# Modulation products placed further behind their loads, and two small jobs moved from VectorE to ScalarE

## The chip, the core and the metric

The kernel runs on one core of a Trainium2 chip. Its engines are TensorE (PE in the rows, with PEld for the loading of its weights), VectorE (DVE), ScalarE (ACT), GpSimd (POOL) and SyncE (SP, whose queue issues the DMAs). The time is in microseconds (us) on the device, from one launch; lower is better.

## The reference

Two layers of a backbone over T = 640 tokens (128 of context and 512 of latents) at width 1024. Each layer modulates a normalised input, mixes tokens by three branches, merges them by gates, and then runs a SwiGLU FFN, modulated in the same way. What matters here are the modulation and one branch:

```python
m = silu(c) @ w_mod[l] + b_mod[l]           # 6 x 1024 columns: shift, scale, gate, twice (adaLN)

def step(s, inp):                            # gated DeltaNet, chunks of 64, forward and backward
    qi, ki, kgi, u, w, ... = inp             # u, w come from the inverse of a triangular matrix
    v_new = u - w @ s                        # product with the state, scaled by a decay
    o = q_scaled @ s + (attn of the chunk) @ v_new
    s = s * decay + ki^T @ v_new
```

There are two copies of the modulation (for context and latents), and the recurrence runs in both directions over the chunks.

## The kernel before

All products are fp32, split in a high and a low part: each weight tile is loaded by SP (`wr`), cast to its high part on ScalarE (`wh`), the rest is taken on GpSimd (`wl`), and TensorE runs three matmuls a product into a PSUM tile `pg`. A matmul of this kind covers 320 tokens. A count of "matmul rows" below is a count of these.

**The order is written by a model clock.** The program is a Python generator that emits all engines' instructions in one pass. Main work (the matmul rows) is emitted as it comes; side work (adaLN products, the inverses and scans of the DeltaNet) stands in coroutines. Each coroutine has a time `cur.t`, from a model of every engine's clock (`tick`), and `pump` emits the next piece of a coroutine between two pieces of main work once the model's TensorE clock plus a hint has reached that time (line 435). A DMA in the model takes its bytes by 3.6e5 a us and 2 us. The engines then run their queues in the order emitted, each in order, with semaphores between them. Most instructions are recorded at one line, L2175, that of the helper that emits them.

**adaLN products** (`mods`, line 686). The first 16 columns' products of layer 0 run at the start of the program. All later ones come in 40 halves: one 1 MB load of `in_wmod` into one tile `S` (in the rows `A<-in_wmod_dram`), then 16 rows of small products (`ps<-A,ct`, 32 matmuls in the trace). Because there is one tile, a half's load can start only when the half before has been read. After two halves ScalarE copies the row out, and `turn` turns it by one matmul (`128x8`) and adds the bias on VectorE. The halves lie at six places: layer 0 columns 16 to 28 (74 to 120 us of the span), 28 to 40 (beside the last scan steps, 543 to 586), 40 to 48 (886 to 910), layer 1 columns 0 to 32 (1030 to 1140), 32 to 40 (1952 to 1979), 40 to 48 (2278 to 2300).

**The inverse** (`delta_inv`) is done per batch on VectorE by eliminating columns one after another (`A<-A` with 128 partitions), with `STREAM_TRANSPOSE` to bring 32x32 blocks in place; small matmuls on TensorE (`ps<-A,A 32x32`) then join the blocks. Batch 0 of each layer is "mixed" (it holds both directions), and for each of its four quarters three copies of 32x256 exchange the blocks, in the same tiles `Nm`, `B`, `X` (lines 1319 to 1321).

**The scan** (`delta_step`, line 1365 on) runs 9 steps a layer with an earlier state. Each multiplies queries and keys by the state `S` on TensorE (`ps<-S,A`, two PSUM tiles), scales both by a decay (`egc`, in the rows `dex`): the first tile by one VectorE instruction of 128x512, the second by four ScalarE activations of 128x128. VectorE then subtracts from the values into `R` (two of 128x256, `A<-A,U`), TensorE multiplies `R` by the inverse (`ps<-A` 64x64), and so on to the new state. The order puts 12 matmul rows between the product with the state and the product of `R`.

**The Hyena branch** runs beside the inverses: its projections go from PSUM through ScalarE (`T<-pg`) to VectorE's convolution (`T<-T,par,T` 128x641), and to DRAM (`hyS<-T`).

Of the kernel before, what the change touches and what calls it, by code (L numbers as in the profile page):

```python
# [12 lines left out]
AF = mybir.ActivationFunctionType  # L13
ALU = mybir.AluOpType
# [4 lines left out]
P = 128  # L19
# [279 lines left out]
class _Net:  # L299
# [386 lines left out]
    def mods(self, l, lo, hi, par=False, hint=0.5, first=False):  # L686

        nc = self.nc  # L690
        if par:
            self.load_par(l)
        if l not in self.mod:
            self.mod[l] = self.p2.tile([P, 2, 48], F32, tag="mod", name=self.nm("mod"))
        mv = self.mod[l]
        pick = self.ident.rearrange("p (g c) -> p g c", g=4)[:, :, 0:2]
        last = None

        def turn(j, row):
            ps = self.ps()  # L700
            nc.tensor.matmul(ps[:, 0:8], row, pick, start=True, stop=True)
            nc.vector.tensor_tensor(out=mv[:, :, j:j + 4], in0=ps[:, 0:8].rearrange("p (g s) -> p s g", g=4),
                                    in1=self.par[l][0][:, None, C_BMOD + j:C_BMOD + j + 4].to_broadcast([P, 2, 4]),
                                    op=ALU.add)

        def add(ps, w, h):
            for k in range(KD // 2):
                for g in range(4):
                    nc.tensor.matmul(ps[32 * g:32 * g + 32, :P], self.ct[4 * h + k], w[g][:, k * P:k * P + P],
                                     start=h + k == 0, stop=h == 1 and k == 3)  # L710

        W = {}
        if first:
            for j in range(lo, hi, 2):
                S = self.A()
                for i in range(2):
                    if j + i == hi - 4:
                        self.wload(1)
                    W[j + i] = S[:, i * D:i * D + D]
                    nc.sync.dma_start(W[j + i], self.I["wmod"][l, j + i])  # L720
        else:
            S = self.A()
        for j in range(lo, hi, 4):
            ps = None
            for h in range(2):
                if first:
                    w = [W[j + g][:, h * 512:h * 512 + 512] for g in range(4)]
                else:
                    w = [S[:, g * 512:g * 512 + 512] for g in range(4)]
                    nc.sync.dma_start(S[:, :2048].rearrange("p (g c) -> p g c", g=4),  # L730
                                      self.I["wmod"][l, j:j + 4, :, h * 512:h * 512 + 512].rearrange("g p c -> p g c"))
                self.on(*w, *([last[1]] if last else []))
                yield hint
                if first and j == lo and not h:
                    self.tables()
                ps = ps or self.ps()
                add(ps, w, h)
                if last:
                    turn(*last)
                    last = None  # L740
            row = self.U()[:, :P]
            nc.scalar.copy(row, ps[:, :P])
            last = j, row
        self.on(last[1])
        yield hint
        turn(*last)
# [506 lines left out]
    def delta_inv(self, N, us):  # L1253

        nc = self.nc
        v = nc.vector
# [32 lines left out]
        for c in range(31, 0, -1):  # L1289
            js = [(c, 32)] if c > 24 else [(c, c + (32 - c) // 2), (c + (32 - c) // 2, 32)]  # L1290
            tv = []
            for a, b in js:
# [3 lines left out]
                                in1=X[:, c:c + 1, a:b].to_broadcast([P, c, w]), op=ALU.mult)  # L1296
# [6 lines left out]
        def unpack(dst, p, a, o2):  # L1303
            q = slice(64 * p + 32 * a, 64 * p + 32 * a + 32)
            src = X[q].rearrange("p r c -> p c r") if not o2 else X[q]
            v.transpose(out=dst.rearrange("p m i -> p i m"), in_=src)

        for p, a in quads:
            q = slice(64 * p + 32 * a, 64 * p + 32 * a + 32)
            bwd = p ^ us[0]  # L1310
            nd = Nm[q, :, 32 * a:32 * a + 32]
            if mixed:
                unpack(nd, p, a, 0)
                yield 1.5
                unpack(B[q], p, a, 1)
                ub = [u for u in range(nu) if p ^ us[u]][0]
                b3 = X[q, 0:8]
                bv, nv = B[q, ub * 8:ub * 8 + 8], nd[:, ub * 8:ub * 8 + 8]
                v.tensor_copy(b3, nv)
                v.tensor_copy(nv, bv)  # L1320
                v.tensor_copy(bv, b3)
            else:
                unpack(nd, p, a, bwd)
                if a == bwd:
                    yield 1.5
                    unpack(B[q], p, a, 1 - bwd)
            yield 0 if (p, a) == quads[-1] else 1.5

        W = S[:, 1024:2048].rearrange("p (m c) -> p m c", c=32)
        for m0 in range(0, nu * 8, 16):  # L1330
            ps = self.ps()
            for m in range(m0, m0 + 16):
                s = us[m // 8]
# [7 lines left out]
            for mm in range(m0, m0 + 16, 8 if mixed else 16):  # L1341
                n = 8 if mixed else 16
                s = us[mm // 8]
# [5 lines left out]
        for m0 in range(0, nu * 8, 16):  # L1349
            ps = self.ps()  # L1350
            for m in range(m0, m0 + 16):
                s = us[m // 8]
# [6 lines left out]
            for mm in range(m0, m0 + 16, 8 if mixed else 16):  # L1359
                n = 8 if mixed else 16  # L1360
                s = us[mm // 8]
# [8 lines left out]
    def delta_step(self, N, Pm, R, St, u, s, t, S, zero):  # L1370

        nc = self.nc
        v = nc.vector
# [8 lines left out]
        if not zero:  # L1382
            pk = [self.ps(), self.ps()]
            for hh in range(4):
                for n, src in enumerate((self.k, self.q)):
                    for h2, par in DIAG:
                        c0 = t * P + par * 64
                        nc.tensor.matmul(pk[h2][halves[par], hh * P + n * 64:hh * P + n * 64 + 64],
                                         src[halves[h2], hh, c0:c0 + 64], S[halves[h2], par ^ s, hh],
                                         start=True, stop=True)  # L1390
            tm = [self.U().rearrange("p (a n d) -> p a n d", a=4, n=2) for _ in range(2)]
            v.tensor_tensor(out=tm[0].rearrange("p a n d -> p a (n d)"), in0=pk[0].rearrange("p (a d) -> p a d", a=4),
                            in1=self.egc[:, s, t, 0, :, None].to_broadcast([P, 4, 128]), op=ALU.mult)
            for hh in range(4):
                nc.scalar.activation(tm[1][:, hh].rearrange("p n d -> p (n d)"), pk[1][:, hh * P:hh * P + P], AF.Copy,
                                     scale=self.egc[:, s, t, 1, hh:hh + 1])
            for h2 in range(2):
                v.tensor_tensor(out=R[:, h2], in0=hv(vt)[:, h2], in1=tm[h2][:, :, 0], op=ALU.subtract)
            nc.gpsimd.tensor_tensor(out=St, in0=S, in1=self.egl[:, s, :, t, :, None].to_broadcast([P, 2, 4, 64]),
                                    op=ALU.mult)  # L1400
        else:
            nc.gpsimd.tensor_copy(R, hv(vt))
        nc.gpsimd.tensor_tensor(out=hv(kg), in0=hv(kt), in1=self.kgf[:, s, t, :, :, None].to_broadcast([P, 2, 4, 64]),
                                op=ALU.mult)
# [821 lines left out]
```

## Time and profile before

| | |
|---|---|
| runs | 2827.09, 2834.18, 2837.05 us; median 2834.18 |
| profiled execution | 2837.89 us, of it 2836.1 in the span |
| mean granted TensorE clock | 0.949 |
| TensorE busy | 2566.9 us, 91% |
| VectorE busy | 1856.7 us, 65% |
| ScalarE busy | 1017.8 us, 36% |
| GpSimd busy | 1332.8 us, 47% |

The busy times are of the one profiled execution, over its whole span; the granted clock is a share of TensorE's full 2.4 GHz, and 0.50 is its lower level of 1.2 GHz.

### The profile page before, as it was taken

What the parts mean: (1) busy time and instruction counts of PE and PEld (TensorE: products, weight loads), DVE (VectorE), ACT (ScalarE), POOL (GpSimd) and SP (SyncE); (2) the same over time, 40 slices, a digit from 0 to 9 for tenths busy, and PEclk for the clock granted to TensorE, in tenths of its full rate; (3) what the DMA queues carried; (4) which work ended last, traced back from release to release, by engine and by line L of the source; (5) the groups of instructions that cost most, each with busy time, mean ns of one, the idle gap of its engine ahead of it and who ended that gap; (6) DMA issues with size and microseconds to landing.
All of it is one profiled execution on the core that took longest, in us unless ns stands there. A gap on an engine that the chain in (4) does not pass through costs nothing. (4 is left out here: it accounts for less than half of the span.)

```text
span 2836.1 us, 55639 instructions
## 1 busy us (share of the span) xinstructions
PE 2566.9 (91%) x22520; PEld 2434.9 (86%) x22520; DVE 1856.7 (65%) x3417; ACT 1017.8 (36%) x2175; POOL 1332.8 (47%) x1228
## 2 busy tenths in 40 slices
PE   5898779788999999999988979698899989999998
PEld 3687779788998888999977778687889989999997
DVE  5466987544654484767665789784555347877765
ACT  4454224232332342433435532332323323444432
POOL 2234426242335464666742444353423345767662
PEclk8999989899999999999999989798999999999999
DMA  7541221333564246222222312213336442222222
GB/s 288 178 143 56 69 77 56 115 120 122 180 234 148 84 129 216 91 81 89 84 84 97 121 54 79 78 58 98 115 138 243 152 156 65 71 83 83 82 75 82
DMA packets 109552, 324.18 MB, mean 114 GB/s; under 512 B 10202, under 2 KB 24538, under 8 KB 102816
## 3 DMA queue, kind: packets, MB, share of 16 engines
q1 hardware_dynamic: 107856, 312.76, 32.8%
q0 software_dynamic: 1440, 7.87, 0.8%
q8 instruction: 177, 2.90, 0.4%
q14 instruction: 79, 0.65, 0.1%
HBM read 288.60 MB, written 37.24 MB: 115 GB/s over the span
## 5 line engine op out<-in xcount | busy, mean ns | idle before, releaser
L2175 PE MATMUL pg<-A,wh 128*128 128x320 f32 (+1 forms) x6304 | 1473.2, 321 | 52.2 <-DVE T L2175 15.3
L2175 PEld LDWEIGHTS pg<-A,wh 128*128 128x128 f32 (+1 forms) x6304 | 1082.0, 194 | 98.1 <-POOL A L2175 18.6
L2175 POOL TENSOR_TENSOR wl<-wr,wh 128x512 fp32r<-128x512 f32 (+2 forms) x486 | 680.0, 1413 | 769.6 <-ACT wh L2175 730.7
L2175 PE MATMUL pg<-A,wl 128*128 128x320 f32 (+1 forms) x3152 | 997.7, 317 | 0.3 <-POOL wl L2175 0.2
L2175 PEld LDWEIGHTS pg<-A,wl 128*128 128x128 f32 (+1 forms) x3152 | 610.2, 194 | 3.6 <-POOL wl L2175 2.7
L2175 ACT CAST wh<-wr 128x512 fp32r<-128x512 f32 (+2 forms) x486 | 286.3, 612 | 442.9 <-PE pg L2175 341.4
L2175 PE MATMUL ps<-A,wh 128*128 128x320 f32 x1696 | 378.0, 309 | 0.0
L2175 PEld LDWEIGHTS ps<-A,wh 128*128 128x128 f32 x1696 | 283.4, 188 | 1.4 <-issue 1.2
L2175 PE MATMUL ps<-A,wl 128*128 128x320 f32 x848 | 262.9, 310 | 4.6 <-POOL wl L2175 4.4
L2175 PE MATMUL ps<-A,A 32*32 32x32 f32 (+5 forms) x2984 | 215.1, 251 | 52.9 <-DVE A L2175 51.0
L2175 POOL TENSOR_TENSOR wl<-U,wh 128x512 fp32r<-128x512 f32 x160 | 226.6, 1432 | 48.0 <-ACT wh L2175 48.0
L2175 PEld LDWEIGHTS ps<-A,A 32*32 32x32 f32 (+2 forms) x2984 | 186.4, 154 | 66.3 <-DVE A L2175 52.2
L2175 DVE TENSOR_TENSOR A<-A 128x120 f32<-128x120 f32 (+22 forms) x690 | 216.1, 375 | 11.0 <-DMA A<-hyS 8.0
L2175 DVE TENSOR_TENSOR T<-T,T 128x320 f32<-128x320 f32 (+1 forms) x139 | 130.3, 937 | 86.0 <-ACT T L2175 81.8
L2175 POOL TENSOR_TENSOR A<-A,A 128x640 fp32r<-128x640 f32 (+5 forms) x84 | 121.0, 1453 | 112.5 <-ACT A L2175 111.6
L2175 PEld LDWEIGHTS ps<-A,wl 128*128 128x128 f32 x848 | 159.2, 188 | 7.0 <-POOL wl L2175 7.0
L2175 PE MATMUL pg<-A,A 128*128 128x320 f32 x1056 | 160.9, 310 | 0.0
L2175 ACT CAST wh<-U 128x512 fp32r<-128x512 f32 x160 | 99.1, 620 | 162.8 <-PE ps L2175 64.2
L2175 PEld LDWEIGHTS pg<-A,A 128*128 128x128 f32 x1056 | 156.1, 188 | 0.7 <-issue 0.2
L2175 DVE STREAM_TRANSPOSE A<-A 32x1024 f32<-32x1024 f32 x72 | 148.9, 2093 | 1.3
L2175 DVE TENSOR_TENSOR U<-ps,U 128x512 f32<-128x512 f32 x144 | 78.0, 543 | 104.2 <-PE ps L2175 66.3
L2175 DVE SCALAR_TENSOR_TENSOR A<-pg,mod,A 128x320 f32<-128x320 f32 (+2 forms) x152 | 72.8, 492 | 84.9 <-PE pg L2175 84.6
(163 smaller groups left out, 3021.1 us busy)
## 6 DMA issues: line engine op xcount, KB each, us to landing
wr<-in_wbig_dram SPq DMA_DIRECT2D x272, 512.0 KB, 3.6
A<-in_wmod_dram SPq DMA_DIRECT2D x40, 1024.0 KB, 5.3
A<-hT SPq DMA_DIRECT2D x32, 1024.0 KB, 7.1
kSp<-U SPq DMA_DIRECT2D x40, 256.0 KB, 2.1
U<-kSp SPq DMA_DIRECT2D x40, 256.0 KB, 6.0
A<-in_wmod_dram SPq DMA_DIRECT2D x16, 512.0 KB, 10.2
hyS<-T SPq DMA_DIRECT2D x24, 320.5 KB, 3.1
wr<-in_wbig_dram SPq DMA_DIRECT2D x16, 384.0 KB, 3.2
```

The source lines that it names most:

```text
L2175: return f(*a, **k)
```

## The change

Three edits. In `mods`, each of the 40 later halves gets 4 us added to its coroutine's time after the model's end of its load, so that its products are emitted further behind the load. In `delta_inv`, the three copies per quarter of a mixed batch go from VectorE to ScalarE (24 instructions). In `delta_step`, the VectorE instruction that scales the first PSUM tile becomes four ScalarE activations, so that ScalarE does eight a step (18 VectorE instructions out, 72 ScalarE instructions in).

```diff
@@ mods
                 self.on(*w, *([last[1]] if last else []))
+                if not first:
+                    self.cur.t += 4.0
                 yield hint
@@ delta_inv
-                v.tensor_copy(b3, nv)
-                v.tensor_copy(nv, bv)
-                v.tensor_copy(bv, b3)
+                nc.scalar.copy(b3, nv)
+                nc.scalar.copy(nv, bv)
+                nc.scalar.copy(bv, b3)
@@ delta_step
-            v.tensor_tensor(out=tm[0].rearrange("p a n d -> p a (n d)"), in0=pk[0].rearrange("p (a d) -> p a d", a=4),
-                            in1=self.egc[:, s, t, 0, :, None].to_broadcast([P, 4, 128]), op=ALU.mult)
-            for hh in range(4):
-                nc.scalar.activation(tm[1][:, hh].rearrange("p n d -> p (n d)"), pk[1][:, hh * P:hh * P + P], AF.Copy,
-                                     scale=self.egc[:, s, t, 1, hh:hh + 1])
+            for h2 in range(2):
+                for hh in range(4):
+                    nc.scalar.activation(tm[h2][:, hh].rearrange("p n d -> p (n d)"), pk[h2][:, hh * P:hh * P + P],
+                                         AF.Copy, scale=self.egc[:, s, t, h2, hh:hh + 1])
```

Since the model clock sets the order, all three edits move instructions. Three places show it.

SyncE's queue at layer 0's columns 40 to 48 (886 to 910 us), before: four loads of adaLN weights (`A`) and the stream's weight loads (`wr`).

```order
L2175 DMA wr_9441<-in_wbig_dram 128x1024
L2175 DMA wr_9507<-in_wbig_dram 128x1024
L2175 DMA A_9509<-in_wmod_dram 128x4x512 x2
L2175 DMA wr_9603<-in_wbig_dram 128x1024
L2175 DMA A_9509<-in_wmod_dram 128x4x512 x2
L2175 DMA wr_9727<-in_wbig_dram 128x1024
```

The same place after the change.

```order
L2176 DMA A_9536<-in_wmod_dram 128x4x512
L2176 DMA wr_9627<-in_wbig_dram 128x1024
L2176 DMA A_9536<-in_wmod_dram 128x4x512
L2176 DMA wr_9714<-in_wbig_dram 128x1024
L2176 DMA A_9536<-in_wmod_dram 128x4x512
L2176 DMA wr_9809<-in_wbig_dram 128x1024
L2176 DMA A_9536<-in_wmod_dram 128x4x512
```

Every adaLN load now has a weight load of the stream between it and the next. On TensorE the four halves stood 30, 24 and 24 matmul rows apart and stand 60, 54 and 54 apart; in layer 0's columns 16 to 28 the first three spacings go from 12, 24 and 30 rows to 42, 48 and 78, the last two from 36 and 66 to 30 and 60; in layer 1's columns 0 to 32 they were 24 to 54 and are 54 to 84; at 2278 to 2300 us as at 886, and at 1952 to 1979 us from 18, 6 and 18 to 24, 24 and 24.

TensorE at the end of layer 0's scan, columns 28 to 40, before: `ps<-A,ct` is an adaLN half, `small,U` its `turn`, `pg` the stream's matmuls, `64x64 x16` a product of the scan.

```order
L2175 MATMUL ps_6293<-A_5907,ct 32x128 x16
L2175 MATMUL pg_6446<-A_449,wh_6065 128x320
L2175 MATMUL pg_6446<-A_451,wh_6065 128x320
L2175 MATMUL pg_6446<-A_449,wl_6066 128x320
L2175 MATMUL pg_6446<-A_449,wh_6065 128x320
L2175 MATMUL pg_6446<-A_451,wh_6065 128x320
L2175 MATMUL pg_6446<-A_449,wl_6066 128x320
L2175 MATMUL ps_6453<-A_4379 64x64 x16
L2175 MATMUL ps_6472<-small,U_6444 128x8
L2175 MATMUL pg_6446<-A_449,wh_6065 128x320
```

The same end after the change, from the scan's last product on.

```order
L2176 MATMUL ps_6578<-U_6556,A_4493 64x64 x16
L2176 MATMUL ps_6442<-A_6041,ct 32x128 x16
L2176 MATMUL ps_6618<-A_6041,ct 32x128 x16
L2176 MATMUL ps_6635<-small,U_6615 128x8
L2176 MATMUL ps_6618<-A_6041,ct 32x128 x16
L2176 MATMUL ps_6657<-small,U_6655 128x8
L2176 MATMUL pg_6661<-A_449,wh_6210 128x320
```

The last three of the six halves now stand behind one another with no matmul row between them, behind the scan instead of beside it. Elsewhere in layer 0 the join of batch 0's inverse moves from 1232 matmul rows after the program's start to 1346, that of batch 1 from 1340 to 1400; in layer 1 both stand 18 rows earlier.

ScalarE in layer 0's mixed inverse, before: casts of the weight stream (`wh<-wr`) and evictions of a Hyena projection (`T<-pg`).

```order
L2175 COPY T_3318<-pg_3324 128x192
L2175 ACTIVATE T_3319<-pg_3324,par_90 128x192
L2175 CAST wh_3393<-wr_3236 128x512
L2175 CAST wh_3397<-wr_3236 128x512
L2175 COPY T_3318<-pg_3367 128x320
L2175 ACTIVATE T_3319<-pg_3367,par_90 128x320
```

The same place after the change, at the first quarter.

```order
L2176 COPY T_3404<-pg_3410 128x192
L2176 ACTIVATE T_3405<-pg_3410,par_90 128x192
L2176 COPY A_2544<-A_2321 32x256
L2176 COPY A_2321<-A_2544 32x8x32
L2176 COPY A_2544<-A_2544 32x256
L2176 CAST wh_3483<-wr_3310 128x512
L2176 CAST wh_3487<-wr_3310 128x512
L2176 COPY T_3404<-pg_3454 128x320
L2176 ACTIVATE T_3405<-pg_3454,par_90 128x320
```

The three copies, the first of which waits for VectorE's `STREAM_TRANSPOSE`, now stand ahead of two casts and of the eviction whose result VectorE's next convolution reads. VectorE's own transposes and eliminations of the next quarter wait for none of the copies.

## Rows read from the trace of the kernel before

**Rows 1.** Waits of TensorE, whole run: engine, tile, releaser: total us, times, longest.
```profile
PE ps L2175 <- DVE A L2175: 64.9, 24, 14.5
PE ps L2175 <- DMA A<-in_wmod_dram: 34.5, 23, 4.7
```

**Rows 2.** The same, of windows 74:120, 543:586, 886:910, 1030:1140, 1952:1979, 2278:2300.
```profile
PE ps L2175 <- DMA A<-in_wmod_dram: 4.5, 3, 3.3
...
PE ps L2175 <- DMA A<-in_wmod_dram: 8.9, 3, 4.7
...
PE ps L2175 <- DMA A<-in_wmod_dram: 5.6, 4, 2.3
...
PE ps L2175 <- DMA A<-in_wmod_dram: 6.6, 8, 1.4
...
PE ps L2175 <- DMA A<-in_wmod_dram: 3.0, 1, 3.0
...
PE ps L2175 <- DMA A<-in_wmod_dram: 6.0, 4, 2.7
```

**Rows 3.** Windows: us, busy PE, PEld, DVE, ACT, POOL, PEclk, DMA share, GB/s.
```profile
84.00:86.00 2.00, 2.00 (x15) 2.00 (x14) 0.00 (x0) 0.97 (x3) 1.13 (x1) 0.97 0.86 299
...
1150.00:1450.00 300.00, 299.68 (x2034) 297.68 (x2034) 208.27 (x338) 115.82 (x218) 188.64 (x136) 1.00 0.27 84
...
1970.00:1972.00 2.00, 2.00 (x57) 1.93 (x49) 0.75 (x2) 0.32 (x1) 1.27 (x1) 0.58 0.88 342
```

**Rows 4.** The same view, layer 0's inverse.
```profile
265.00:390.00 125.00, 96.75 (x929) 92.04 (x928) 122.69 (x268) 30.55 (x72) 50.98 (x66) 0.88 0.24 76
```

**Rows 5.** Timeline of TensorE there, the join of batch 0.
```profile
384.40 1.73 PE L2175 MATMUL ps<-A,A 32*32 32x32 f32 x62 [13.16 <-DVE A L2175]
```

**Rows 6.** Timeline, loads (SPq) and products: start, duration, count, [idle before, releaser].
```profile
75.56 0.38 SPq L2175 DMA_DIRECT2D A<-in_wmod_dram  x1
...
80.68 1.94 PE L2175 MATMUL ps<-A,ct 128*32 128x128 f32 x32 [3.31 <-DMA A<-in_wmod_dram]
...
552.58 0.37 SPq L2175 DMA_DIRECT2D A<-in_wmod_dram  x1
...
559.82 1.94 PE L2175 MATMUL ps<-A,ct 128*32 128x128 f32 x32 [4.75 <-DMA A<-in_wmod_dram]
...
1965.27 1.93 PE L2175 MATMUL ps<-A,ct 128*32 128x128 f32 x32 [2.97 <-DMA A<-in_wmod_dram]
```

**Rows 7.** Lines by form, whole run (`wh`, `T`: 280:460): count, busy us, mean ns, idle before.
```profile
L2175 DVE COPY A<-A 32x256 f32<-32x256 f32 x24 | 9.4, 391 | 0.8
...
L2175 ACT COPY A<-ps 32x256 f32<-32x256 f32 x8 | 2.9, 363 | 18.5 <-PE ps L2175 18.4
...
L2175 ACT CAST wh<-wr 128x512 fp32r<-128x512 f32 x28 | 16.9, 620 | 39.7 <-PE pg L2175 26.6 <-DMA wr<-in_wbig_dram 12.2 <-issue 0.8
...
L2175 DVE TENSOR_TENSOR U<-ps,dex 128x512 f32<-128x512 f32 x18 | 12.4, 687 | 52.1 <-PE ps L2175 52.0
...
L2175 ACT ACTIVATE T<-pg,par 128x320 f32<-128x320 f32 x9 | 4.8, 535 | 0.0
```

**Rows 8.** Timeline, two scan steps: DVE, ACT and PE at 540, DVE and POOL at 550.
```profile
540.12 0.69 DVE L2175 TENSOR_TENSOR U<-ps,dex 128x512 f32<-128x512 f32 x1 [11.58 <-PE ps L2175]
540.85 0.92 DVE L2175 TENSOR_TENSOR A<-A,U 128x256 f32<-128x256 f32 x2
...
540.16 1.15 ACT L2175 ACTIVATE U<-ps,dex 128x128 f32<-128x128 f32 x4 [2.57 <-PE ps L2175]
...
541.98 1.15 PE L2175 MATMUL ps<-A 64*64 64x64 f32 x32
...
550.52 2.73 DVE L2175 TENSOR_TENSOR A<-A,U 128x256 f32<-128x256 f32 x2
...
551.56 2.82 POOL L2175 TENSOR_TENSOR wl<-wr,wh 128x512 fp32r<-128x512 f32 x2
```

**Rows 9.** Waits of ScalarE, 340:460.
```profile
ACT wh L2175 <- DMA wr<-in_wbig_dram: 12.2, 2, 6.9
```

## The prediction

> **What bounds the kernel now.** The table of busy times comes first: TensorE works 91% of the span, no other engine above 65%. So a microsecond counts where TensorE stands idle, or where it runs at the lower clock after standing. The view of TensorE's waits is next. The largest named entry is for VectorE's tiles `A`, 64.9 us in 24 waits; the second is for the adaLN loads, 34.5 us in 23 waits [rows 1]. Both are touched by the change. The same view cut by place puts the adaLN waits at 4.5, 8.9, 5.6, 6.6, 3.0 and 6.0 us in the six places in which halves run [rows 2]. In between, TensorE hardly waits: 299.68 us busy of 300 from 1150 on, in 2034 matmuls, so that one matmul row of the stream is worth 299.68/2034 = 0.147 us [rows 3]. VectorE is the limit in one kind of stretch: in layer 0's inverse it is busy 122.69 of 125 us while TensorE is busy 96.75 [rows 4], and the join of batch 0 stands 13.16 us for it [rows 5].
>
> I forecast by terms against the profiled execution's own 2837.9 us; the median of the runs shown is 3.7 us lower, and I take that off at the end.
>
> **Term 1: adaLN waits outside the scan of layer 0.** The timeline gives the time that a half needs from its load's issue to its product: 75.56 to 80.68 is 5.1 us, 552.58 to 559.82 is 7.2 us [rows 6]. Halves 24 rows apart give only 24 x 0.147 = 3.5 us, so a wait of some 2 us is what the spacing before must cost. After the change most stand 54 to 84 rows apart, 7.9 to 12.3 us, which is more than either load took. The five places other than the scan's lose 4.5 + 5.6 + 6.6 + 3.0 + 6.0 = 25.7 us [rows 2]. Two of them also lose clock. After the wait that ends at 80.68 [rows 6] the granted clock over 84 to 86 is 0.97 [rows 3], so the lower level lasts until about 84.1: 3.4 us at half rate cost 1.7 us. After 1965.27 [rows 6] it is still 0.58 over 1970 to 1972 [rows 3], so full rate returns at about 1971.7, and 6.4 us at half rate cost 3.2 us. Together -30.6 us. The matmul rows that now fill the gaps are not new work; they come from behind, where they were needed for nothing by then. Where spacing stays short (42 rows are 6.2 us, 30 are 4.4) up to 1.0 and 2.8 us can stay; so the bounds are -26 to -31, and I take the lower end, since most places are beyond 7.2 us.
>
> **Term 2: the halves at the end of layer 0's scan.** Before, three waits cost 8.9 us [rows 2], two of them long (4.75 is one [rows 6]), each followed by a slow stretch like the 3.2 us above: some 15.3 us. After, the last three halves stand back to back. One tile holds the weights, so the second and third load start only when the half before has been read, and nothing else is in TensorE's queue to run: 2 x 5.1 = 10.2 us idle. The slow clock costs about 0.9 us on the product between and 3.2 us behind, and the last `turn` must wait for ScalarE's copy, some 0.8 us: 15.1 us. So the term is 0. With loads of 7.2 us it is +4; with one of them begun earlier than I think it is -2. This is a new wait that takes the place of an old one.
>
> **Term 3: layer 0's inverse.** Twelve copies of 0.391 us leave VectorE [rows 7], which is the limit there: -4.7 us. The join of batch 1 has 60 more matmul rows ahead of it, 60 x 0.147 = 8.8 us that fill part of the 13.16 us gap [rows 5]: -8.8. Against that stands ScalarE's queue. The three copies wait for VectorE's transpose, and two casts and an eviction stand behind them; VectorE's next convolution reads that eviction. A 32x256 copy on ScalarE from SBUF is not in the trace; the nearest are 0.363 us from PSUM and VectorE's 0.391 [rows 7], which bound it closely. So VectorE can stand for 3 x 0.36 + 2 x 0.62 + about 0.95 (two instructions like the 0.535 [rows 7] and a shorter one) = 3.3 us. In two of the four quarters the convolution comes soon enough to meet this: +6.6. Sum -6.9; between -13.5 (no standing) and 0 (no filling).
>
> **Term 4: layer 1's inverse.** Again -4.7 us of copies, but 18 rows fewer ahead of the joins (+2.6) and one quarter that stands (+3.3): +1.2, between -4.7 and +5.9.
>
> **Term 5: the 18 scan steps.** VectorE's scaling took 0.687 us, and VectorE had stood idle 52.1 us before these instructions [rows 7]: taking them off it saves nothing. In the step at 540 both engines began together, ScalarE's four took 1.15 us, `R` was done at 540.85 + 0.92 = 541.77, and TensorE came for it at 541.98 without a wait [rows 8]. With eight activations in a row the first tile is scaled at about 541.3 and the second at about 542.4 (twice 1.15 less a little overlap); the second half of `R` then ends near 542.9, 0.9 us after TensorE arrives. The 12 rows between are the same in the new order. That is 18 x 0.9 = 16 us at most. In a step such as that at 550, where GpSimd runs beside it, `R` took 2.73 us [rows 8]; there the second half is ready before the first is through, and the delay is only that of the first tile, 0.5 us. I take 0.5 for each step: +9 us; ends 0 and 16.
>
> A page speaks against this edit: the Trainium skill's "Perfetto Trace Analysis" (Optimizing Scalar/DVE Operations) advises moving work to ScalarE when VectorE is saturated. By that rule the copies should move and the scalings should not; the trace agrees on both, with the 122.69 of 125 us and the 52.1 us above.
>
> Sum: -30.6 + 0 - 6.9 + 1.2 + 9.0 = -27.3, so 2810.6 for an execution like the profiled one, and 2806.9 against the median: 2807 us.
>
> **Rivals.**
>
> Given back: the waits go, but the scans and inverses return it. Terms -26, +4, 0, +5.9, +16: 0 us, so 2834. For it speaks that the step at 540 had only 0.2 us of slack; against it that it needs every term at its bad end.
>
> Loads late: each adaLN load now has a `wr` load ahead of it in SyncE's queue, which may itself wait for a buffer, so the lead on paper is not the lead of the load. If half of term 1 stays, the sum is -15.3 - 6.9 + 1.2 + 9 = -12, and the time 2822. Against it: before, the loads at 75.56 and 552.58 were issued as their tile came free.
>
> No contention: the slow `R` at 550 ran beside GpSimd's work. If that is what made it 2.73 instead of 0.92 us [rows 8], a later start could fall behind GpSimd's products and `R` be fast again, so that term 5 is 0: sum -36.3, time 2798. Against it: GpSimd's next work follows at 551.56 for 2.82 us [rows 8], just when the later `R` would run. The Trainium skill's "SBUF — State Buffer" (SBUF: two separate sides) has a rule of this kind: VectorE with two SBUF inputs and GpSimd take one port pair in turn, each for a whole instruction.
>
> Slower: ScalarE's order becomes the limit of the inverses. Copies wait for VectorE, casts wait behind the copies, and a cast can wait for its weight load too, which ScalarE did for 12.2 us in two waits in this stretch [rows 9], 3 us a quarter. Then VectorE stands 3.3 to 6.3 us in each of the eight quarters, 26 to 50 us. With no filling, -30.6 - 9.4 + 2.6 + 16 = -21.4 besides, so +5 to +29, in the middle +17: 2851 us. It decides from 2.7 us a quarter on. For it: VectorE has no slack there. Against: much of its work in a quarter is elimination, which waits for no eviction.
>
> **How the numbers follow.** Forecast 0.53, own range 2790 to 2824; no contention 0.15; loads late 0.10; given back 0.12; slower 0.10. About 8.5 us (0.3%) is what the runs can tell from no change. Faster: 0.53 + 0.15 + 0.08 of the late loads = 0.76. Same: given back and the rest, 0.14. Slower 0.10. The range goes from 2786 (terms 3 and 5 near their good ends) to 2836, which takes in the given-back case and leaves out most of the slower one.
>
> **What would show it.** TensorE's waits for adaLN loads should fall from 34.5 to 10 to 15 us, with the two long ones left at the end of layer 0's scan and hardly any at the other places. VectorE's busy time should fall by about 22 us (9.4 + 12.4), ScalarE's rise by about 29. The wait of the product of `R` for VectorE should appear in the scan steps, 0.5 us each. In the inverse, VectorE should stand 3 us before a convolution in two or three quarters, and the 13.16 us gap should be near 5. I am wrong if the adaLN waits stay above 20 us, if VectorE's idle time in the inverses exceeds 20 us, or if the scan steps cost over 1 us each.

## The result and the profile after

| | before | after |
|---|---|---|
| median of runs | 2830.64 us (2819.91 to 2837.48, 6 runs) | 2787.01 us (2786.0 to 2788.38, 6 runs) |
| ratio | | 0.9852, 95% interval 0.9836 to 0.9869 |
| profiled execution's span | 2836.1 us | 2786.2 us |
| VectorE busy in it | 1856.7 us | 1838.5 us |
| ScalarE busy in it | 1017.8 us | 1043.0 us |

The change takes 42 us off (1.48%; "us off" here and below is the ratio's share of 2830 us). The forecast was 27 us off, 2807; its own range was 2790 to 2824, and the whole range went down to 2786. The profiled execution of before was near the top of its own runs (2837.89; later, on other chips, its median was 2826 to 2830), so that some 8 us of the 50 between the two traces is the execution, not the change.

VectorE is busy 18 us less, ScalarE 25 us more, as forecast (22 and 29) but for a few us. TensorE's waits after, over the whole run:

```profile
PE ps L2176 <- DVE A L2176: 35.7, 30, 3.9
...
PE pg L2176 <- ACT T L2176: 17.9, 8, 3.9
...
PE ps L2176 <- DMA A<-in_wmod_dram: 10.0, 2, 5.3
```

Against [rows 1], the adaLN waits fell from 34.5 to 10.0 us, the ones for VectorE's `A` from 64.9 to 35.7, the longest from 14.5 to 3.9. One entry is new: `pg <- ACT T`, 17.9 us, where it had been 4.0. TensorE there reads Hyena projections that ScalarE evicts.

The two adaLN waits left are those at the end of layer 0's scan (TensorE's timeline; of the three halves that stand back to back the first starts at 572.90, the others wait):

```profile
579.32 1.94 PE L2176 MATMUL ps<-A,ct 128*32 128x128 f32 x32 [5.34 <-DMA A<-in_wmod_dram]
...
586.41 1.94 PE L2176 MATMUL ps<-A,ct 128*32 128x128 f32 x32 [4.63 <-DMA A<-in_wmod_dram]
```

And the granted clock behind them stays at its lower level until about 594.6 (columns as in [rows 3]):

```profile
592.00:594.00 2.00, 2.00 (x9) 2.00 (x9) 1.76 (x8) 0.00 (x0) 0.00 (x0) 0.50 0.00 0
594.00:596.00 2.00, 2.00 (x14) 2.00 (x13) 1.76 (x7) 0.44 (x1) 0.00 (x0) 0.85 0.00 0
```

The two joins of the mixed batches, against [rows 5] and its like in layer 1 (14.53 us):

```profile
390.86 1.35 PE L2176 MATMUL ps<-A,A 32*32 32x32 f32 x48 [3.16 <-DVE A L2176]
...
1760.02 1.10 PE L2176 MATMUL ps<-A,A 32*32 32x32 f32 x62 [2.11 <-ACT A L2176]
```

What has come in their place stands earlier, in TensorE's queue at the projections, and in VectorE's before the convolutions:

```profile
367.16 0.90 PE L2176 MATMUL pg<-A,wh 128*128 128x320 f32 x2 [3.59 <-ACT T L2176]
```

```profile
350.41 3.75 DVE L2176 SCALAR_TENSOR_TENSOR T<-T,par,T 128x641 f32<-128x641 f32 x2 [3.17 <-POOL wl L2176]
...
368.98 2.84 DVE L2176 SCALAR_TENSOR_TENSOR T<-T,par,T 128x641 f32<-128x641 f32 x2 [2.68 <-POOL wl L2176]
...
393.87 3.06 DVE L2176 SCALAR_TENSOR_TENSOR T<-T,par,T 128x641 f32<-128x641 f32 x2 [2.25 <-POOL wl L2176]
```

Layer 1 has one of each that is as long (3.53 us at 1747.10, 2.63 at 1748.92). How the waits at 367.16 and 368.98 come about is seen in ScalarE's rows at 364: it waits 11.64 us for VectorE's transpose with the copies at the head of its queue, and the evictions follow only then.

```profile
364.64 1.27 ACT L2176 COPY A<-A 32x256 f32<-32x256 f32 x3 [11.64 <-DVE A L2176]
...
366.67 0.44 ACT L2176 ACTIVATE T<-pg,par 128x192 f32<-128x192 f32 x1
```

TensorE runs on at 367.16, right behind the last of these evictions, and VectorE, whose idle time the view puts down to GpSimd's `wl`, at 368.98, behind the next ones.

A scan step after the change, against [rows 8] (VectorE, ScalarE, GpSimd):

```profile
568.33 0.43 DVE L2176 TENSOR_TENSOR A<-A,U 128x256 f32<-128x256 f32 x1 [3.15 <-ACT U L2176]
...
569.36 0.43 DVE L2176 TENSOR_TENSOR A<-A,U 128x256 f32<-128x256 f32 x1 [0.60 <-ACT U L2176]
...
567.15 2.17 ACT L2176 ACTIVATE U<-ps,dex 128x128 f32<-128x128 f32 x8 [5.45 <-PE ps L2176]
...
566.63 1.04 POOL L2176 TENSOR_TENSOR U<-A,dex 128x512 f32<-128x512 f32 x1
...
569.84 0.68 PE L2176 MATMUL ps<-A 64*64 64x64 f32 x16 [0.23 <-DVE A L2176]
```

Eight activations take 2.17 us, as worked out. But in this step the subtractions start when GpSimd has done its two products (the second of them is shown; its next work begins at 569.91), and take 0.43 us each; TensorE waits 0.23 us, not 0.9. Over all steps the lines by form give

```profile
L2176 DVE TENSOR_TENSOR A<-A,U 128x256 f32<-128x256 f32 x36 | 22.3, 625 | 76.3 <-ACT U L2176 76.2
```

where it had been 891 ns in the mean (30.9 us).

To place the difference I took the time at which TensorE has done a given number of the stream's matmuls, in both traces ("the stream's time" below). After against before, this is -5.7 us behind the first adaLN place, -12.9 behind layer 0's inverses, -17.7 behind its scan, -24.1 behind columns 40 to 48, -33 behind layer 1's first halves, -38 behind layer 1's inverses and most of its scan, -45 behind columns 32 to 40, -49.9 at the end. Single executions differ by some us at each place.

### The profile page after: what moved, and what is told of

It reads as the page before. It is cut to its first block, busy times and chain, and to the rows that moved or that the text cites. A ratio compares the mean times of both kernels' runs of the same rounds, so it can differ in the third digit from the quotient of the medians.

```text
span 2786.2 us, 55705 instructions
## 1 busy us (share of the span) xinstructions
PE 2559.9 (92%) x22520; PEld 2431.1 (87%) x22520; DVE 1838.5 (66%) x3375; ACT 1043.0 (37%) x2271; POOL 1337.2 (48%) x1228
## 5 line engine op out<-in xcount | busy, mean ns | idle before, releaser
L2176 PE MATMUL pg<-A,wh 128*128 128x320 f32 (+1 forms) x6304 | 1474.3, 321 | 66.4 <-ACT T L2176 17.9
L2176 PEld LDWEIGHTS ps<-A,A 32*32 32x32 f32 (+2 forms) x2984 | 184.7, 151 | 38.3 <-DVE A L2176 17.9
L2176 DVE SCALAR_TENSOR_TENSOR T<-T,par,T 128x641 f32<-128x641 f32 x84 | 106.6, 1270 | 45.3 <-POOL wl L2176 27.1
## 6 DMA issues: line engine op xcount, KB each, us to landing
A<-in_wmod_dram SPq DMA_DIRECT2D x16, 512.0 KB, 10.2
```

The costliest lines, as they stand in the source:

```text
L2176: return f(*a, **k)
```

## The experiments

Ratios are to the kernel before, run on the same chip, with their 95% intervals. The first three take one edit each.

**The delay alone.** Only the added line in `mods`.

> Only the delayed adaLN products; copies and scalings as before. Theory (the waits for the loads are the largest part, and the move of the inverse in the order comes with the delay): 30 to 38 us less than before, adaLN waits of TensorE near 10 us, the 13-us wait of batch 0's join smaller. Rival (the three edits share the gain, the inverse needs the copies moved): under 25 us less, joins still waiting 13 to 15 us in both layers.

2775.74 us, ratio 0.9812 (0.9793 to 0.9831): 53 us off, more than the three edits together, and more than the 30 to 38 expected. The adaLN waits fell to 5.5 us. The rival is out as to the size. But its second half holds, in both layers: TensorE still waits 14.5 us for the join in layer 1, and as long for that of batch 0 in layer 0:

```profile
387.08 1.15 PE L2177 MATMUL ps<-A,A 32*32 32x32 f32 x40 [14.03 <-DVE A L2177]
```

So the delay alone shortens neither, although in layer 0 it moves batch 0's inverse by 96 matmul rows in the order and batch 1's by 60 (in layer 1 it moves none). The stream's time still gains 11 us over layer 0's inverses. Two waits for GpSimd's tile `U`, 5.8 us together before, are gone with the delay and still there with the copies alone; the rest of the 11 is not placed.

**The copies alone.**

```diff
-                v.tensor_copy(b3, nv)      # and the two after it
+                nc.scalar.copy(b3, nv)
```

> Only the 24 copies on ScalarE. Theory (VectorE is the limit of the inverses, so its 4.7 us a layer come off): 6 to 10 us less than before, the two joins 4 to 5 us earlier each. Rival (ScalarE's queue holds casts and evictions, VectorE stands for them): no change or up to 10 us more, VectorE idle over 5 us a layer in the inverse.

2819.04 us, 0.997 (0.9956 to 0.9984): 8 us off. The joins' waits go from 13.16 to 0.89 and from 14.53 to 3.65 us, and TensorE's waits for VectorE's `A` from 64.9 to 35.9, but its waits for ScalarE's `T` rise:

```profile
PE ps L2175 <- DVE A L2175: 35.9, 22, 4.7
...
PE pg L2175 <- ACT T L2175: 17.3, 8, 5.2
...
PE ps L2175 <- ACT A L2175: 14.5, 7, 5.5
```

So both are at work: VectorE's queue is shorter, 29.0 us less waiting for its `A`, and ScalarE's, held by the copies, gives 13.3 us of it back as waits for `T`, and 5.9 as waits for the tiles `A` that ScalarE writes (8.6 before). The 9.8 us left are about the 8 that the time shows.

**The scaling alone.**

> Only the scaling of both product tiles on ScalarE. Theory (the later subtractions run after GpSimd's two products and take 0.43 us each instead of 0.9, which pays for the longer scaling): within 4 us of before, subtractions 0.65 us in the mean. Rival (0.5 us a step added, as forecast): 7 to 12 us more.

2832.66 us, 1.0028 (1.001 to 1.0046): 8 us slower, with 3 and 13 as the ends of the interval. Six of the ten runs took 2828 to 2833 us and four 2842 to 2844. The subtractions do take less (633 ns in the mean), as the theory had it. The size is the rival's, the forecast's +9. Its mechanism is not in the trace: TensorE's waits for the product of `R` are 3.9 us in all, against 5.5 before, and in this one pair of traces the stream takes 3 to 5 us less than before over either scan. Where the 8 us arise is not shown.

**GpSimd's products held beside the subtractions.** The changed kernel, and ahead of the product `St`:

```diff
+            nc.gpsimd.tensor_copy(St[:, 0, 0, 0:1], tm[0][:, 3, 1, 63:64])
             nc.gpsimd.tensor_tensor(out=St, in0=S, ...
```

> The changed kernel, but GpSimd's two products of each scan step are held by one small copy that reads the last scaled part of the first tile, so that they run beside VectorE's subtractions again. Theory (the two engines keep each other waiting): subtractions go from 0.63 back to 0.9 us or more in the mean, and the kernel is 4 to 16 us slower than the changed one. Rival (the subtractions were slow for another reason): mean stays under 0.7 us and the time within 4 us of the changed kernel.

2783.98 us, 0.9845 (0.983 to 0.9859), the same as the changed kernel; the mean is 638 ns. In its step at 570 the held products began at 571.53, after the first subtraction (570.98, 0.42 us) was done, so this run made only half of the case that it was meant to make. The second subtraction ran beside the held product, and was slow again:

```profile
572.02 0.83 DVE L2177 TENSOR_TENSOR A<-A,U 128x256 f32<-128x256 f32 x1 [0.61 <-ACT U L2177]
...
571.53 1.04 POOL L2177 TENSOR_TENSOR A<-S,dex 128x512 f32<-128x512 f32 x1
```

It ended 0.28 us after the product did, and TensorE waited 0.65 us for it. Over all steps TensorE's waits for the product of `R` are 9.9 us, against 4.6 in the changed kernel, without a longer time.

**Delay and copies**, scaling as before.

> Delay and copies, scaling as before. Theory (the scaling costs some 8 us, and the pair delay and copies loses what the back-to-back halves at the end of layer 0's scan cost): ratio 0.981 to 0.984, 2 to 10 us under the changed kernel, adaLN waits about 10 us in two. Rival (parts add up): ratio near 0.978, 62 us under before.

2781.95 us, 0.9851 (0.9822 to 0.988): the same as all three edits: the theory's gain of 2 to 10 us does not show, and the rival's 62 us is out. The parts do not add up: delay 53 and copies 8 off, together 42. The wait for adaLN loads is 11.9 us in three waits, against 5.5 in the delay alone. The stream's time against the delay alone shows where: about equal before layer 0's scan (1 us ahead at 1800 matmuls), 12 us behind after it. The copies cost time on ScalarE in the model clock that writes the order: two of layer 0's three joins move a further 18 and 42 rows, and one more half is left over at the end of the scan, back to back.

**All three, with a shorter delay beside layer 0's scan.**

```diff
-                    self.cur.t += 4.0
+                    self.cur.t += 1.0 if l == 0 and lo == 28 else 4.0
```

> All three edits, but a delay of 1.0 instead of 4.0 for the halves beside layer 0's scan, which puts 12 to 18 matmul rows between them and none back to back. Theory (two loads in a row with nothing between, and the slow clock behind them, are what the full change loses there): 4 to 12 us under the changed kernel. Rival (the waits only move into the scan): within 3 us of the changed kernel, adaLN waits 8 to 10 us again.

2778.21 us, 0.9833 (0.9812 to 0.9854); adaLN waits 2.6 us. In the stream's time it is 1 us behind the delay alone over that scan, where the changed kernel is 12 behind. The 5 us between the ratios' middles lie within the intervals, so the loss is read from the traces: adaLN waits down from 10.0 to 2.6 us, and 11 us less over that stretch.

**The delay alone, 2.0 beside layer 0's scan.**

> The delay alone, with 2.0 instead of 4.0 beside layer 0's scan: halves 18, 18, 18, 18 and 30 matmul rows apart, none back to back. Theory: 0 to 8 us under the delay alone, adaLN waits under 3 us. Rival: the same as the delay alone within 3 us, since the one long wait there is covered by what follows.

2767.78 us, 0.9801 (0.9769 to 0.9833), adaLN waits 0.9 us. Lower in the middle than the delay alone, not separated from it, so the rival stands as well.

**Delay and copies, 1.0 there.**

> Delay and copies, with 1.0 instead of 4.0 beside layer 0's scan: 12, 12, 18, 18 and 0 rows apart, so one pair back to back instead of two. Theory: 4 to 8 us under delay and copies, the fastest of all at a ratio of 0.979 or below. Rival (the copies gain nothing once the delay has moved layer 0's inverse): as the delay alone, 0.981.

2774.94 us, 0.9819 (0.9791 to 0.9847). One back-to-back half less, 9 us faster in the middle than delay and copies, though the intervals overlap, and no faster than the delay alone. The rival stands: with the delay, the copies' move in both layers is worth nothing that can be measured.

**Copies in layer 1 alone**, with the delay of 2.0.

```diff
+                cp = nc.scalar.copy if self.mixes > 1 else v.tensor_copy
+                cp(b3, nv)                 # and the two after it; self.mixes counts mixed batches
```

> Delay alone with 2.0 beside layer 0's scan, and the copies on ScalarE in layer 1 only. Theory (with the delay in place the copies' move gains nothing in layer 0, and 5 to 10 us in layer 1, where the order of the inverse is not moved by the delay): ratio 0.976 to 0.978, the fastest so far. Rival (the copies gain in neither): 0.980, as without them.

2767.09 us, 0.9778 (0.9757 to 0.9798). The middle is lower than without the copies by 6 us; the intervals overlap.

**GpSimd's products held behind the subtractions**, scaling on both engines as before:

```diff
+            nc.gpsimd.tensor_copy(St[:, 0, 0, 0:1], R[:, 1, 3, 63:64])
             nc.gpsimd.tensor_tensor(out=St, in0=S, ...
```

> Delay alone with 2.0 beside layer 0's scan, scaling on both engines as before, but GpSimd's two products of each scan step held by one small copy that reads the finished second half of R. Theory (VectorE and GpSimd keep each other waiting): the subtractions fall from 0.75 to 0.45 to 0.65 us in the mean, time within 6 us of the kernel without the hold, since the products now end 2 us later. Rival (no such waiting): the mean stays at 0.7 to 0.9 us.

2759.86 us, 0.9764 (0.9741 to 0.9786). The subtractions' row:

```profile
L2178 DVE TENSOR_TENSOR A<-A,U 128x256 f32<-128x256 f32 x36 | 17.8, 502 | 1.9
```

502 ns in the mean, from 790 in the same kernel without the hold. That settles the point that the earlier hold left half open. In this run 31 of the 36 ran with no GpSimd instruction beside them, and each took 0.41 to 0.43 us; before, 12 did, again at 0.41 to 0.43, and most of the other 24 took 0.9 to 1.5. The Trainium skill's "SBUF — State Buffer" (SBUF: two separate sides) says that a VectorE instruction with two SBUF inputs and a GpSimd one that reads SBUF take one port pair in turn, for a whole instruction, and the row agrees with that. What it is worth in time, 10 us between the ratios, is not separated from none.

**The delay everywhere but beside layer 0's scan.**

> The delay at all places but beside layer 0's scan, copies and scalings as before. Theory (the gain outside the scan is the waits taken out, 31 us with the clock): 31 to 45 us under before, adaLN waits of 4 to 9 us left, all at the scan. Rival (the delay at the scan is itself worth much): under 30 us.

2779.55 us, 0.9829 (0.9807 to 0.985): 48 us off (31 to 45 expected), adaLN waits 4.7 us, at the scan. So the five other places and the moved order give nearly all that the delay alone gives.

**The two gains put together**: copies in layer 1, products held.

> Delay with 2.0 beside layer 0's scan, GpSimd's products held behind the subtractions, and the copies on ScalarE in layer 1 only. Theory (the copies gain 5 to 8 us in layer 1): ratio 0.973 to 0.975, below the 0.9764 of the same kernel without the copies' move. Rival (the copies gain nothing once the waits are gone): 0.976 to 0.978.

2755.22 us, 0.9742 (0.972 to 0.9764): 73 us off the kernel before, and 31 us, about 1.1%, below the changed kernel by the ratios. The copies' part (0.9764 to 0.9742) is in the middle as the theory had it, but the intervals overlap.

## Why the prediction came out as it did

The direction and the largest term were right; the sum was 15 us short. The time lies below the forecast's own range of 2790 to 2824, and the whole range held it by 1 us. That is luck: its end of 2786 stood for good ends of terms 3 and 5, of which only term 5's came. Between the sum and the two traces, 23 us apart, some 9 are term 5, 6 are term 4 and 3 to 5 are term 2.

**Term 1, -30.6.** Right. The stream's time falls by 5.7 us at the first place (6.2 forecast), by 4.7 at columns 40 to 48 (5.6), 7 at layer 1's first halves (6.6), 8 around columns 32 to 40 (6.2, with some scan steps in it) and 5 at the last (6.0): some 31 us. The run with the delay everywhere but at the scan has no wait left at any of them.

**Term 2, 0.** The mechanism was right and the idle time too: 5.34 + 4.63 = 10.0 us for the 10.2 forecast, and the clock low until 594.6. The price was compared with the wrong thing. Against before, the stretch from the first scan steps to 620 us gained 3 to 5 us; at least 3.13 us of it is a wait for VectorE at 614.90 in the trace of before, just behind the scan, that has no like in the trace after. Against what the delay could give, this is a loss of some 10 us: all three edits with the shorter delay there, which leaves no halves back to back, have hardly any of it.

**Term 3, -6.9.** It measured -7.2 in layer 0's inverses, but the agreement is luck. VectorE stood 3.17, 2.68 and 2.25 us before convolutions, 8.1 in all (6.6 forecast, in two quarters, not three). The join's wait fell by 10.0 us, and not by filling: the 60 rows are batch 1's and the gap is batch 0's, and with the delay alone, 96 rows later, that gap is 14.03 us, while with the copies alone it is 0.89. Part of it came back in a place that I had not named: TensorE itself waits on ScalarE's evictions, 3.59 us at 367.16 and the like. Nor do the two sides add: over this stretch the delay alone gains 11 us, the copies alone 8, and all three edits 7. (The upper end, given as 0 for no filling, should have been +1.9.)

**Term 4, +1.2.** Mis-sized: -4 to -5 in the stream's time across layer 1's inverses and scan. I charged 2.6 us for 18 matmul rows fewer ahead of the joins. Before, though, TensorE stood 14.53 us at that join; fewer rows ahead of a wait cost nothing while the wait lasts. What sets that time is VectorE's chain: the join starts 37.9 us earlier (1797.94 to 1760.02) where the stream ahead of it was 32.7 earlier, which is 5.2 us, about the 4.7 of the copies. With the delay alone the two are 46.4 and 46.3, so that nothing is left for the join.

**Term 5, +9.** This is the step that failed. TensorE does wait for `R` in the scan steps after, as forecast, but less: 14 waits of 0.16 to 0.72 us, 4.6 us in all. And before, it had waited 5.5 us already, 4.4 of them in two steps that I had not looked at, at 406 and 1883 us, where the subtractions ran beside GpSimd's `wl`:

```profile
405.17 2.67 POOL L2175 TENSOR_TENSOR wl<-wr,wh 128x512 fp32r<-128x512 f32 x2 [1.96 <-ACT wh L2175]
405.29 2.83 DVE L2175 TENSOR_TENSOR A<-A,U 128x256 f32<-128x256 f32 x2
406.87 0.68 PE L2175 MATMUL ps<-A 64*64 64x64 f32 x16 [1.55 <-DVE A L2175]
```

These two are gone after, so the new small waits and the old long ones cancel. The rival named "no contention", at 0.15 and 2798 us, is what happened to the instruction: the subtractions fell to 625 ns. By itself, however, the scaling costs 8 us, close to the 9 forecast though not by these waits; with the delay and copies it costs nothing that can be measured (0.9851 without it, 0.9852 with it). Why that is so is not settled. The order around the steps differs in the two, and the runs that would hold it fixed were not made.

The rivals: "loads late" is out, as no place outside the scan waits. "Slower" named the mechanism that does give back part of the copies' gain (waits for `T` from 4.0 to 17.9 us), 13.9 us for its 26 to 50. VectorE's eliminations going on under it, as the forecast's argument against it had it, may be why; no run isolates that. "Given back" did not come about in total, but in a form that I had not listed: one edit took part of what another gave, by way of the written order.

## What to carry to other kernels

When a program's order is written by a model clock, a delay that is right at five places can pile up work at a sixth: print the order at the forced end, and give that place its own number (here 11 us in the traces, not separated in the time). Price a step that is moved to another engine by what stands behind it in that engine's queue, as well as by what it frees; here, of 29.0 us of freed waiting, 13.3 came back as waits for evictions and 5.9 as waits for the copies' engine. And test edits one at a time: here the largest alone beat all three together.

## What the runs showed that I had not expected

VectorE's subtraction of 128x256 takes 0.43 us with GpSimd idle and up to 1.5 with it at work, and both ways to take the two apart get the 0.43: a later start of the subtraction (20 of 36 in the changed kernel), or holding GpSimd's products (31 of 36).
